# Four instead of three buffers for gathered rows, and three fewer key units computed ahead, in the expert layer of a fused two-block kernel

## The chip, the cores and the metric

One Trainium2 chip, one of its cores. The metric is the device time of one execution in microseconds; lower is better. The engines are named as the profile names them: PE multiplies matrices (PEld is its weight load), DVE works on vectors, ACT computes activations and copies, POOL issues the gathers here, SP issues the plain loads from memory.

## The reference

The program is a hybrid block (pooling and forgetting attention), a second block of two attentions, and then an expert layer (PEER) over 512 tokens of width 1024. All that the change touches lies in the expert layer, which is, cut to what matters:

```python
def block(xt):                                   # 128 tokens at a time
    q = (xt @ w_q).reshape(128, 8, 2, 128)
    sc = einsum('thcd,chnd->thcn', q, sub_keys)  # 8 heads, 2 x 128 sub-keys
    ...                                          # top 16 of each, top 16 of their sums
    g = softmax(best_s)                          # 8 x 16 experts of 16384 per token
    pre = einsum('td,thkd->thk', xt, u[idx])
    coef = g * gelu(pre)
    return einsum('thk,thkd->td', coef, v[idx])
```

`u` and `v` are tables of 16384 rows of 1024 numbers.

## The kernel before

The expert layer treats its tokens in two ways, side by side.

**The first 128 tokens** take their expert rows by gathers. For each of the 128 selected slots, `gather_load` (L1613) lets POOL issue an indirect load of one row of `u` or of `v` per token (128 rows of 4 KB, 512 KB) into a tile `gat`. `gather_step` (L1622) lets DVE use it: a `u` row is multiplied with the token and summed (L1631, into `pre`), a `v` row is scaled and added to `acc` (L1635). That makes 256 gathers and 256 DVE steps. The list `items` alternates `v` and `u` after the first 24 `u`. A step that has used its tile issues the next load at once, so that as many gathers are under way as `gat` has buffers; a load waits until the DVE step that last used its buffer is done.

**The other 384 tokens** are computed against all 16384 experts, 128 experts to a unit. A *u stage* (`u_stage`, L1395) is 24 PE matmuls of 384 columns, in three passes over a high and a low part of the operands; ACT applies Gelu (`u_gelu`, L1445) and leaves the result in a *slot*, a tile of 128 x 384 numbers. A *v stage* (`v_half`, L1717, twice) multiplies the unit's weights with the `v` rows: 18 matmuls of 512 columns, added up in six banks over all 128 units. Ahead of each stage `prep` (L1378) splits the loaded tile into its high part on ACT (L1389: `uhi`, `h_hi`, `vhi`) and its low part on DVE (L1390: `ulo`, `h_lo`, `vlo`), and has SP load the next tile (L1364). Two sets of tiles take turns, so the same work shows as `uhi`/`ulo` and as `h_hi`/`h_lo`.

The program's order is written by hand. Each engine runs its instructions in that order.

1. *Routing* (until about 963 us): queries, top-16 searches, and in between 22 of the u stages, then 3 more.
2. *One-hots* (about 972 to 1119 us): 24 blocks (`one_hots` L1649 on DVE: `aa`, `oh` and two `bb`; `products` L1662 on PE: 32 small matmuls, copied by ACT) build a table of gate weights `Gd` in memory. A block may hold one u stage; the number per block follows from `left`, what is still to be computed ahead.
3. Five further u stages, each with a gather step.
4. *The main loop* (L1739, about 1140 to 2010 us): 128 turns, each with one v stage. `NU` u stages are done ahead of it, the other 128 - `NU` inside, in the turns that `u_at` lists (at most one per turn, from turn 5 to turn 122). This is the loop, cut:

```python
gdue = float(after)                       # after = 5 gather steps are done
for s in range(128):
    if s in u_at:
        o = u_stage(u_at[s])
    gdue += 2.9 if s in u_at else 0.75
    if s + 1 in u_at:
        prep("u", u_at[s + 1], V)
    ...                                   # gate_load every 8 turns; w_mult, prep("v"), w_split for turn s + 1
    if s in u_at:
        u_gelu(u_at[s], o)
    v_half(s, 0)
    while gi["use"] < min(int(gdue), len(items)):
        gather_step()
    v_half(s, 1)
```

So DVE's order in a turn is: the low part for the next u stage, the weights (L1705, L1712) and the low part for the next v stage, and then the gather steps that have come due. `gate_load` (L1699) has SP fetch 1.5 MB of `Gd` for eight turns. The slots are `NU` in number: 10 `Gx`, 10 `Gm`, 16 `Gn`, `Gq`, two PSUM banks and three parts of a gate tile. `Gq` and `gat` lie in one pool (`pQ`) in SBUF. After the loop the rows of the other 384 tokens are read back (`xr`, in `gat`'s buffers) and added to the banks.

Of the kernel before, what the change touches and what calls it, by code (L numbers as in the profile page):

```python
# [10 lines left out]
F32 = mybir.dt.float32  # L11
# [12 lines left out]
D = 1024  # L24
# [36 lines left out]
def hybrid_mla_peer_kernel(ctx: ExitStack, tc: tile.TileContext, x, meta, gains, rows, bforget, wf, w1v, w1u, poolw,  # L61
# [13 lines left out]
    def bank(tag, bufs):  # L75
        return ps.tile([128, 512], F32, name=tag, tag=tag, bufs=bufs)
# [1241 lines left out]
    ND = T - 128  # L1318
# [17 lines left out]


    FIRST = 5
    NU = 20 + 16 + 13 + FIRST
    ahead_of = list(range(FIRST, NU)) + list(range(FIRST))  # L1340
    LEAD = 122
    done = [min(128, NU + (max(0, s + 2 - FIRST) * (128 - NU)) // (LEAD + 2 - FIRST)) for s in range(128)]
    u_at = {s: done[s] - 1 for s in range(128) if done[s] > (done[s - 1] if s else NU)}
    assert all(done[s] >= min(128, s + 4) for s in range(128)) and len(u_at) == 128 - NU
    VA = 1
# [49 lines left out]
    def u_stage(j):  # L1395
        o = mm_bank()
        hi, lo = uw.pop(j)
        for k in range(KD):
            mm3(o[:, :ND], (hi[:, k, :], lo[:, k, :]), (h3[0][:, k, 128:T], h3[1][:, k, 128:T]), k == 0, k == KD - 1)
        return o  # L1400
# [38 lines left out]
    slots = [Gx[:, i, :] for i in range(10)] + [Gm[:, i, :] for i in range(10)]  # L1439
# [3 lines left out]
    def u_gelu(j, o):  # L1443
        gl[j] = slots.pop(0)
        S.activation(gl[j], o[:, :ND], AF.Gelu)  # L1445

    def run_ahead(n, eng):
        for _ in range(n):
            i = ua["n"]
            ua["n"] += 1  # L1450
            if i + 1 < NU:
                prep("u", ahead_of[i + 1], eng)
# [138 lines left out]
        by_slot(tt)  # L1591
    cR.close()
    pQ = ctx.enter_context(tc.tile_pool(name="pQ", bufs=1))
    Gq = pQ.tile([128, 13, ND], F32, name="Gq", tag="Gq")
    slots.extend(Gq[:, i, :] for i in range(13))
    slots.extend(bank(tag, 1)[:, :ND] for tag in ("av", "mi"))


# [14 lines left out]
    def gather_load():  # L1613
        if gi["load"] < len(items):
            kind, s = items[gi["load"]]
            t = pQ.tile([128, D], F32, name="gat", tag="gat", bufs=3)
            G.indirect_dma_start(out=t, out_offset=None, in_=peer_u if kind == "u" else peer_v,  # L1617
                                 in_offset=bass.IndirectOffsetOnAxis(ap=idx[:, s:s + 1], axis=0))
            gt[gi["load"]] = t
            gi["load"] += 1  # L1620

    def gather_step():  # L1622
        i = gi["use"]
        if i >= len(items):
            return
        kind, s = items[i]
        while gi["load"] <= i:
            gather_load()
        t = gt.pop(i)
        if kind == "u":  # L1630
            V.tensor_tensor_reduce(t, t, xt0, 1.0, 0.0, op0=OP.mult, op1=OP.add, accum_out=pre[:, s:s + 1])  # L1631
            if s % 16 == 15:
                ripe.append((i + LATE, s // 16))
        else:
            V.scalar_tensor_tensor(acc, t, pre[:, s:s + 1], acc, op0=OP.mult, op1=OP.add)  # L1635
        gi["use"] += 1
        gather_load()
        if ripe and ripe[0][0] <= i:
            h = ripe.pop(0)[1]
            c = pre[:, 16 * h:16 * h + 16]  # L1640
            S.activation(c, c, AF.Gelu)
            V.tensor_tensor(c, c, gg0[:, h, :], op=OP.mult)

    for _ in range(3):
        gather_load()


# [29 lines left out]
    n_b = ND // NB  # L1677
    left = NU - after - ua["n"]
    for b in range(n_b + 1):
# [16 lines left out]
    def gate_load(q):  # L1696
        if q < 128 // GJ:
            gates[q] = tV([128, ND // NB, GJ * NB], "gate", bufs=2)
            nc.sync.dma_start(gates[q], Gd[q])  # L1699

    def w_mult(j):
        g = gates[j // GJ].rearrange("p b (j t) -> p b j t", j=GJ)[:, :, j % GJ, :]
        x = gl.pop(j)
        xv = x.rearrange("p (b t) -> p b t", t=NB)
        V.scalar_tensor_tensor(xv, xv, 1.0 / 16384.0, g, op0=OP.mult, op1=OP.mult)  # L1705
        return x

    def w_split(j, x):
        hi = tV([128, ND], "w_hi", F32R, bufs=2)
        lo = tV([128, ND], "w_lo", F32R, bufs=2)  # L1710
        S.activation(hi, x, AF.Copy)  # L1711
        V.tensor_tensor(lo, x, hi.bitcast(F32), op=OP.subtract)  # L1712
        if j >= FIRST:
            slots.append(x)
        return hi, lo

    def v_half(j, n):  # L1717
        hi, lo = vw[j]
        w = ws[j]
        c = slice(512 * n, 512 * n + 512)  # L1720
        for tt in range(3):
            mm3(ob[2 * tt + n], (w[0][:, tok(tt)], w[1][:, tok(tt)]), (hi[:, c], lo[:, c]), j == 0, j == 127)
        if n == 1:
            vw.pop(j), ws.pop(j)
# [13 lines left out]
    gdue = float(after)  # L1738
    for s in range(128):  # L1739
        nx = s + VA  # L1740
        if s in u_at:
            o = u_stage(u_at[s])
        gdue += 2.9 if s in u_at else 0.75
        if s + 1 in u_at:
            prep("u", u_at[s + 1], V)
        if nx < 128:
            if nx == FIRST or nx % GJ == 0:
                gate_load(nx // GJ + 1)
            wg = w_mult(nx)
            prep("v", nx, V)  # L1750
            ws[nx] = w_split(nx, wg)
# [6 lines that stand above are left out]
# [2 lines left out]
        gather_step()  # L1760
    xr = []
    for tt in range(3):
        xr.append(pQ.tile([128, D], F32, name="xr", tag="gat", bufs=3))
        nc.scalar.dma_start(xr[tt], x2d[tt])
    nc.scalar.dma_start(out[0:128, :], acc)
    for n in range(2):
# [81 lines left out]
```

## Time and profile before

| what | value |
|---|---|
| time, median of 3 runs | 2022.4 us (2020.04 to 2023.79) |
| the profiled execution's own time | 2023.68 us |
| its span, first to last instruction | 2020.9 us |
| PE busy | 1951.3 us, 97% |
| DVE busy | 1370.9 us, 68% |
| ACT busy | 770.8 us, 38% |
| POOL busy | 619.5 us, 31% |
| granted TensorE clock, mean | 0.986 |

A busy PE is not a PE at its peak: the profile models the ends of matmuls, which overlap. What a stage of matmuls takes is therefore read from the starts of the first one of it and of the next stage, and what PE loses from the idle time ahead of an instruction and from the clock. Granted clock 1.0 is 2.4 GHz, 0.5 is 1.2 GHz.

### The profile page before, as it was taken

What the parts mean: (1) busy time and instruction counts of PE and PEld (TensorE: products, weight loads), DVE (VectorE), ACT (ScalarE), POOL (GpSimd) and SP (SyncE); (2) the same over time, 40 slices, a digit from 0 to 9 for tenths busy, and PEclk for the clock granted to TensorE, in tenths of its full rate; (3) what the DMA queues carried; (4) which work ended last, traced back from release to release, by engine and by line L of the source; (5) the groups of instructions that cost most, each with busy time, mean ns of one, the idle gap of its engine ahead of it and who ended that gap; (6) DMA issues with size and microseconds to landing.
All of it is one profiled execution on the core that took longest, in us unless ns stands there. A gap on an engine that the chain in (4) does not pass through costs nothing.

```text
span 2020.9 us, 26905 instructions
## 1 busy us (share of the span) xinstructions
PE 1951.3 (97%) x10297; PEld 1669.7 (83%) x10297; DVE 1370.9 (68%) x2571; ACT 770.8 (38%) x1228; POOL 619.5 (31%) x479
## 2 busy tenths in 40 slices
PE   7999999999997989999999999999999999999998
PEld 5777688877886779889999888888888888888887
DVE  4233423564576668999899677777787777777686
ACT  4223323254575442223565433333333333333332
POOL 1001100200147015655100134434444444433442
PEclk9999999999999999999999999999999999999999
DMA  4211122322111133213789888888888888888885
GB/s 156 92 63 42 42 84 96 133 92 73 36 54 63 42 133 108 94 42 105 231 260 264 277 321 319 315 304 296 321 288 304 302 310 292 313 318 306 282 293 205
DMA packets 138129, 387.63 MB, mean 192 GB/s; under 512 B 10624, under 2 KB 59904, under 8 KB 129808
## 3 DMA queue, kind: packets, MB, share of 16 engines
q1 hardware_dynamic: 48576, 216.65, 30.4%
q0 software_dynamic: 36864, 134.23, 19.4%
q10 hardware_dynamic: 52560, 35.03, 5.9%
q8 instruction: 80, 1.31, 0.3%
q14 instruction: 49, 0.40, 0.1%
HBM read 357.04 MB, written 28.84 MB: 191 GB/s over the span
## 4 chain that ended last, share of the span: by engine, by line
PE 51%; DMA 22%; issue 10%; DVE 9%; POOL 6%; ACT 2%; DVEq 0%; POOLq 0%; ACTq 0%; SPq 0%
DMA gat<-in_peer_v,idx 12%; DMA gat<-in_peer_u,idx 9%; PE mm L150 9%; PE mm L152 9%; PE mm L151 9%; POOL gat L1617 4%; DVE acc L1635 2%; PE s L151 2%; PE s L152 2%; PE s L150 2%; PE pt L151 2%; PE pt L152 2%; PE pt L150 2%; PE av L1044 1%; PE s L561 1%
## 5 line engine op out<-in xcount | busy, mean ns | idle before, releaser
L1617 POOL DMA_INDIRECT gat<-in_peer_u,idx x128 | 203.1, 1586 | 413.2 <-DVE pre L1631 207.0
L1617 POOL DMA_INDIRECT gat<-in_peer_v,idx x128 | 172.6, 1348 | 233.6 <-DVE pre L1631 137.5
L1631 DVE CUSTOM_DVE_ANT_0 gat<-gat,xt 128x1024 f32<-128x1024 f32 x128 | 156.0, 1221 | 102.3 <-DMA gat<-in_peer_u,idx 102.2
L1635 DVE SCALAR_TENSOR_TENSOR acc<-gat,pre,acc 128x1024 f32<-128x1024 f32 x128 | 164.2, 1283 | 83.3 <-DMA gat<-in_peer_v,idx 82.8
L152 PE MATMUL mm<-h_hi,ulo 128*128 128x384 f32 x568 | 192.5, 339 | 7.3 <-DVE ulo L1390 5.9
L150 PE MATMUL mm<-h_hi,uhi 128*128 128x384 f32 x568 | 193.4, 340 | 0.0
L151 PE MATMUL mm<-h_lo,uhi 128*128 128x384 f32 x568 | 191.9, 338 | 0.0
L130 DVE TENSOR_TENSOR wlo<-wraw,whi 128x2048 fp32r<-128x2048 f32 (+1 forms) x42 | 96.1, 2289 | 135.3 <-ACT whi L129 135.2
L152 PE MATMUL mm<-h_hi,h_lo 128*128 128x384 f32 x456 | 156.8, 344 | 16.4 <-DVE h_lo L1390 13.9
L1389 ACT ACTIVATE vhi<-xt 128x1024 fp32r<-128x1024 f32 x97 | 102.7, 1058 | 181.9 <-issue 112.8
L150 PE MATMUL mm<-h_hi 128*128 128x384 f32 x456 | 157.0, 344 | 0.0
L151 PE MATMUL mm<-h_lo,h_hi 128*128 128x384 f32 x456 | 155.6, 341 | 0.0
L129 ACT ACTIVATE whi<-wraw 128x2048 fp32r<-128x2048 f32 (+2 forms) x53 | 97.5, 1841 | 110.9 <-PE mm L151 59.0
L1390 DVE TENSOR_TENSOR vlo<-xt,vhi 128x1024 fp32r<-128x1024 f32 x97 | 118.4, 1221 | 23.2 <-ACT vhi L1389 22.8
L152 PEld LDWEIGHTS mm<-h_hi,ulo 128*128 128x128 f32 x568 | 107.7, 190 | 9.3 <-DVE ulo L1390 7.2
L150 PEld LDWEIGHTS mm<-h_hi,uhi 128*128 128x128 f32 x568 | 107.6, 190 | 1.8
L151 PEld LDWEIGHTS mm<-h_lo,uhi 128*128 128x128 f32 x568 | 107.7, 190 | 1.7
L150 PE MATMUL mm<-hT_hi,whi 128*128 128x512 f32 x256 | 104.7, 409 | 1.3 <-DVE fz L417 1.0
L150 PE MATMUL s<-vhi,w_hi 128*128 128x512 f32 x256 | 100.0, 391 | 4.5 <-ACT w_hi L1711 4.5
L152 PEld LDWEIGHTS mm<-h_hi,h_lo 128*128 128x128 f32 x456 | 87.8, 192 | 19.6 <-DVE h_lo L1390 16.6
L152 PE MATMUL mm<-hT_hi,wlo 128*128 128x512 f32 x256 | 102.2, 399 | 0.0
L151 PE MATMUL mm<-hT_lo,whi 128*128 128x512 f32 x256 | 102.1, 399 | 0.0
(586 smaller groups left out, 5062.4 us busy)
## 6 DMA issues: line engine op xcount, KB each, us to landing
xt<-in_peer_v SPq DMA_DIRECT2D x97, 512.0 KB, 5.6
xt<-in_uT SPq DMA_DIRECT2D x95, 512.0 KB, 4.8
Gd<-stage ACTq DMA_DIRECT2D x24, 1024.0 KB, 5.3
gate<-Gd SPq DMA_DIRECT2D x16, 1536.0 KB, 10.4
raw<-in_uT SPq DMA_DIRECT2D x33, 512.0 KB, 4.9
wraw<-in_w1u SPq DMA_DIRECT2D x16, 1024.0 KB, 4.8
raw<-in_peer_v SPq DMA_DIRECT2D x31, 512.0 KB, 5.5
wraw<-in_wpq SPq DMA_DIRECT2D x8, 1024.0 KB, 4.8
```

Of the source, the lines that this page charges most:

```text
L129: S.activation(hi[:, :n], r[:, :n], AF.Copy)
L130: lo_eng["e"].tensor_tensor(lo[:, :n], r[:, :n], hi[:, :n].bitcast(F32), op=OP.subtract)
L150: PE.matmul(o, L[0], R[0], start=start, stop=False)
L151: PE.matmul(o, L[0], R[1], start=False, stop=False)
L152: PE.matmul(o, L[1], R[0], start=False, stop=stop)
L561: PE.matmul(s[:, :w], qT[pr, h // 2, tok(qt)], kT[pr, h // 2, n0:16 + n], start=True, stop=False)
L1044: PE.matmul(av[:, col(h, qt):col(h, qt) + 64], pts[i][:, c + j * 128:c + (j + 1) * 128], src[:, j, h * 64:(h + 1) * 64], start=(j == 0), s ...
L1389: S.activation(hi, src, AF.Copy)
L1390: eng.tensor_tensor(lo, src, hi.bitcast(F32), op=OP.subtract)
L1617: G.indirect_dma_start(out=t, out_offset=None, in_=peer_u if kind == "u" else peer_v, in_offset=bass.IndirectOffsetOnAxis(ap=idx[:, s:s + ...
L1631: V.tensor_tensor_reduce(t, t, xt0, 1.0, 0.0, op0=OP.mult, op1=OP.add, accum_out=pre[:, s:s + 1])
L1635: V.scalar_tensor_tensor(acc, t, pre[:, s:s + 1], acc, op0=OP.mult, op1=OP.add)
```

## The change

```diff
-    NU = 20 + 16 + 13 + FIRST
+    NU = 20 + 16 + 10 + FIRST
...
-    Gq = pQ.tile([128, 13, ND], F32, name="Gq", tag="Gq")
-    slots.extend(Gq[:, i, :] for i in range(13))
+    Gq = pQ.tile([128, 10, ND], F32, name="Gq", tag="Gq")
+    slots.extend(Gq[:, i, :] for i in range(10))
...
-            t = pQ.tile([128, D], F32, name="gat", tag="gat", bufs=3)
+            t = pQ.tile([128, D], F32, name="gat", tag="gat", bufs=4)
...
-    for _ in range(3):
+    for _ in range(4):
         gather_load()
...
-        gdue += 2.9 if s in u_at else 0.75
+        gdue += 2.9 if s in u_at else 0.6
...
-        xr.append(pQ.tile([128, D], F32, name="xr", tag="gat", bufs=3))
+        xr.append(pQ.tile([128, D], F32, name="xr", tag="gat", bufs=4))
```

`gat` gets a fourth buffer of 4 KB per partition. `Gq` gives up three slots of 1.5 KB each for it, so 51 units instead of 54 are computed ahead and 77 instead of 74 u stages lie in the main loop. A turn without a u stage brings 0.6 instead of 0.75 gather steps. With `NU` = 54 all 24 one-hot blocks hold a u stage; with 51, three of them (the first, the ninth and the seventeenth) hold none.

DVE at the first one-hot block, where `g` are the gate weights of the tokens, in the change's order against that before:

```order
 L1588 SCALAR_TENSOR_TENSOR g_5759<-pt,g_5759 128x256
 L1588 SCALAR_TENSOR_TENSOR g_5759<-s,g_5759 128x256
+L1656 TENSOR_TENSOR aa<-I_5757,iota 128x2048
+L1657 TENSOR_TENSOR oh<-J_5758,iota 128x2048
+L1659 TENSOR_TENSOR bb<-oh,g_5759 128x2048 x2
 L1390 TENSOR_TENSOR ulo<-xt,uhi 128x1024
 L1656 TENSOR_TENSOR aa<-I_5757,iota 128x2048
```

The first block's `aa`, `oh` and `bb` now come without a `ulo` ahead of them; the same three rows without a `ulo` stand at the ninth and the seventeenth block.

ACT at the same place, from the last u stage ahead of the blocks on (`Gn<-mm` is `u_gelu`, the four copies and the load to `Gd` are `products`), before:

```order
L1445 ACTIVATE Gn<-mm 128x384
L1389 ACTIVATE h_hi<-raw 128x8x128
L1445 ACTIVATE Gn<-mm 128x384
L1671 COPY stage<-s 128x128x4
L1671 COPY stage<-pt 128x128x4
L1671 COPY stage<-s 128x128x4
L1671 COPY stage<-pt 128x128x4
L1672 DMA Gd<-stage 128x16x128
L1389 ACTIVATE uhi<-xt 128x1024
```

and in the change:

```order
L1445 ACTIVATE Gn<-mm 128x384
L1671 COPY stage<-s 128x128x4
L1671 COPY stage<-pt 128x128x4
L1671 COPY stage<-s 128x128x4
L1671 COPY stage<-pt 128x128x4
L1672 DMA Gd<-stage 128x16x128
L1389 ACTIVATE h_hi<-raw 128x8x128
L1445 ACTIVATE Gn<-mm 128x384
```

One split (`h_hi`) and the Gelu of one u stage stood ahead of the first block's copies and now stand behind them, so one u stage fewer lies ahead of the first `products`.

DVE in turns 10 and 11 of the main loop, from `w_mult` (L1705) of turn 10 on, before:

```order
L1705 SCALAR_TENSOR_TENSOR Gx<-Gx,gate 128x384
L1390 TENSOR_TENSOR vlo<-xt,vhi 128x1024
L1712 TENSOR_TENSOR w_lo<-Gx,w_hi 128x384
L1631 ISA gat,pre<-gat,xt 128x1024
L1631 ISA pre 128x1
L1631 ISA gat,pre<-gat,xt 128x1024
L1631 ISA pre 128x1
L1631 ISA gat,pre<-gat,xt 128x1024
L1631 ISA pre 128x1
L1390 TENSOR_TENSOR ulo<-xt,uhi 128x1024
L1705 SCALAR_TENSOR_TENSOR Gx<-Gx,gate 128x384
L1390 TENSOR_TENSOR vlo<-raw,vhi 128x1024
```

and in the change, from the split for turn 11's u stage on:

```order
L1390 TENSOR_TENSOR h_lo<-xt,h_hi 128x8x128
L1705 SCALAR_TENSOR_TENSOR Gx<-Gx,gate 128x384
L1390 TENSOR_TENSOR vlo<-raw,vhi 128x1024
L1712 TENSOR_TENSOR w_lo<-Gx,w_hi 128x384
L1631 ISA gat,pre<-gat,xt 128x1024
L1631 ISA pre 128x1
L1631 ISA gat,pre<-gat,xt 128x1024
L1631 ISA pre 128x1
L1631 ISA gat,pre<-gat,xt 128x1024
L1631 ISA pre 128x1
L1705 SCALAR_TENSOR_TENSOR Gx<-Gx,gate 128x384
L1390 TENSOR_TENSOR vlo<-xt,vhi 128x1024
```

Turn 11 has a u stage in the change and had none before, so its `h_lo` stands in turn 10 now; the next u stage after turn 10 was that of turn 12, whose `ulo` came behind turn 10's three gather steps. POOL issues the same gathers in the same order. What differs there is the DVE step that a gather's buffer waits for: the third step before it until now, the fourth with the change.

## Rows read from the trace of the kernel before

**Rows 1.** The page, part 4: the chain that ended last, by line.

```profile
DMA gat<-in_peer_v,idx 12%; DMA gat<-in_peer_u,idx 9%; PE mm L150 9%; PE mm L152 9%; PE mm L151 9%; POOL gat L1617 4%; DVE acc L1635 2%; PE s L151 2%; PE s L152 2%; PE s L150 2%; PE pt L151 2%; PE pt L152 2%; PE pt L150 2%; PE av L1044 1%; PE s L561 1%
```

**Rows 2.** Busy time by stretch; last columns clock, DMA share, GB/s.

```profile
core 0: us, PE busy (x) PEld busy (x) DVE busy (x) ACT busy (x) POOL busy (x), PEclk, DMA share, GB/s
1140.00:2010.00 870.00, 845.62 (x4062) 746.12 (x4061) 655.71 (x839) 300.79 (x411) 367.76 (x249) 0.99 0.85 298
985.00:1110.00 125.00, 125.00 (x1167) 121.86 (x1165) 122.32 (x106) 75.09 (x126) 0.00 (x0) 1.00 0.92 263
```

**Rows 3.** Waits of PE, main loop: total us, times, longest.

```profile
PE mm L152 <- DVE h_lo L1390: 13.9, 8, 3.0
PE mm L152 <- DVE ulo L1390: 5.9, 4, 2.5
PE s L150 <- ACT w_hi L1711: 4.5, 3, 3.0
```

**Rows 4.** The same view for DVE, 1155 to 2010 us.

```profile
DVE gat L1631 <- DMA gat<-in_peer_u,idx: 102.2, 47, 8.3
DVE acc L1635 <- DMA gat<-in_peer_v,idx: 82.8, 48, 6.0
```

**Rows 5.** The tile gat, 1155 to 2010 us: idle time until, and landing.

```profile
  DVE acc L1635: 225.6, 87
  DVE pre L1631: 172.4, 58
...
DMA to landing us min/median/max: 4.1/6.2/13.6
```

**Rows 6.** Timelines of DVE, SP, POOL and PE, 1447 to 1468 us.

```profile
1447.87 1.29 DVE L1635 SCALAR_TENSOR_TENSOR acc<-gat,pre,acc 128x1024 f32<-128x1024 f32 x1 [0.44 <-DMA gat<-in_peer_v,idx]
...
1452.31 0.60 SPq L1699 DMA_DIRECT2D gate<-Gd  x1
...
1453.78 1.01 POOL L1617 DMA_INDIRECT gat<-in_peer_v,idx  x1 [2.21 <-DMA gat<-in_peer_v,idx]
...
1465.15 1.28 DVE L1635 SCALAR_TENSOR_TENSOR acc<-gat,pre,acc 128x1024 f32<-128x1024 f32 x1 [6.04 <-DMA gat<-in_peer_v,idx]
...
1467.63 0.55 PE L152 MATMUL mm<-h_hi,h_lo 128*128 128x384 f32 x1 [3.04 <-DVE h_lo L1390]
```

**Rows 7.** Busy time by stretch: a gate load, three clock spells.

```profile
1453.00:1465.00 12.00, 11.59 (x56) 9.83 (x54) 5.11 (x8) 3.04 (x5) 2.87 (x3) 1.00 1.02 414
1116.20:1119.60 3.40, 3.40 (x26) 3.40 (x24) 0.00 (x0) 2.42 (x5) 0.00 (x0) 0.51 0.72 207
1362.00:1365.40 3.40, 3.40 (x13) 3.40 (x12) 3.40 (x6) 1.03 (x2) 1.39 (x1) 0.50 0.86 298
1915.00:1918.40 3.40, 3.40 (x9) 2.51 (x9) 2.88 (x5) 1.82 (x2) 1.39 (x1) 0.50 0.79 266
```

**Rows 8.** Timeline of PE: starts of v, u and v stage.

```profile
1701.40 0.39 PE L150 MATMUL s<-vhi,w_hi 128*128 128x512 f32 x1
...
1705.52 0.33 PE L150 MATMUL mm<-h_hi,uhi 128*128 128x384 f32 x1
...
1709.70 0.39 PE L150 MATMUL s<-vhi,w_hi 128*128 128x512 f32 x1
```

**Rows 9.** Timelines of PE and DVE in one one-hot block.

```profile
1052.75 0.42 PE L150 MATMUL mm<-h_hi 128*128 128x384 f32 x1
...
1055.29 1.23 DVE L1390 TENSOR_TENSOR ulo<-xt,uhi 128x1024 fp32r<-128x1024 f32 x1
...
1056.43 1.22 DVE L1656 TENSOR_TENSOR aa<-I,iota 128x2048 f16<-128x2048 f16 x1
...
1061.31 1.23 DVE L1390 TENSOR_TENSOR h_lo<-xt,h_hi 128x1024 fp32r<-128x1024 f32 x1
```

**Rows 10.** Timeline of PE, the last one-hot block.

```profile
1114.34 0.23 PE L1670 MATMUL s<-bb,aa 128*128 128x128 f16 x1 [1.14 <-DVE bb L1659]
```

**Rows 11.** The page, part 6: one load, KB each, us to landing.

```profile
gate<-Gd SPq DMA_DIRECT2D x16, 1536.0 KB, 10.4
```

## Prediction

> **What bounds the kernel now.** I read the chain of waits first. A quarter of the chain that ended last is the gathers: their transfers 21%, their issue on POOL 4%; the rest of its large entries is matmuls [rows 1]. So two things are near a limit in the main loop, and the busy time by stretch says which: PE is busy for 845.6 of 870 us [rows 2]. PE sets the loop, and the gathers cost time only where they make PE wait. Who waited for whom on PE names those places: 15 waits, 13.9 + 5.9 + 4.5 = 24.3 us, all for the low or high part of an operand (`h_lo`, `ulo`, `w_hi`), none longer than 3.0 us [rows 3]. DVE makes those parts, and the same view for DVE shows it waiting 102.2 + 82.8 = 185 us for the gathers' landing [rows 4]. Most of the 185 us is free, because DVE works about one turn ahead of PE; 24.3 us of it come through.
>
> One event shows how [rows 6]. At 1452.31 SP issues the gate load (1.5 MB, 10.4 us to land [rows 11]). At 1453.78 POOL issues a gather; it lands 11.3 us later, where the median is 6.2 and the longest 13.6 [rows 5]. DVE waits 6.04 us for it at 1465.15, does `h_lo` only then, and PE has waited 3.04 us. In that stretch the DMA engines are full (share 1.02, 414 GB/s) [rows 7], while over the loop they move 298 GB/s at a share of 0.85 [rows 2]. So a late gather is one whose transfer falls into the queue behind a gate load, and there is one such load per eight turns.
>
> A wait on PE costs twice. After the longer ones the granted clock is at 0.50, the 1.2 GHz level, for 3.4 us; six such spells lie in the loop, the first and the last of them in [rows 7]. Half of 3.4 us is lost in each: 6 x 1.7 = 10.2 us. What the gathers cost now is 24.3 + 10.2 = 34.5 us.
>
> **The change, part by part.**
>
> *The fourth buffer.* A gather waits for the DVE step that last used its buffer; POOL waited 225.6 + 172.4 = 398 us for such steps in 145 waits [rows 5], so the buffers, not POOL, set when a gather starts. A turn with a u stage takes 1705.52 - 1701.40 = 4.1 us for the v stage and 1709.70 - 1705.52 = 4.2 us for the u stage [rows 8], 8.3 us in all, and has about three gather steps. With three buffers, and three steps in the turn before as well, each gather is issued when the same step of that turn is done, so it has 8.3 us to land. With four, the first of the three has a whole turn more, and the other two have one DVE step more (1.3 us, the length of the step in [rows 6]), about 9.6 us. DVE's lead adds 6.04 - 3.04 = 3.0 us before PE feels it [rows 6]. So PE waited where a landing took over 11.3 us, and will where it takes over 12.6. Many gathers gain more than 1.3 us: the one of 1453.78 would have had its buffer when the step of 1447.87 ended, at 1449.16, ahead of the gate load instead of behind it. Against that, the longest landing of 13.6 us still exceeds 12.6, and one more gather under way makes each somewhat slower. Bounds: none of the 34.5 us goes (the queue is full anyway), or all. I take 20 of the 24.3 us, leaving 4.3 us or about 0.3 us for each of the 16 gate loads, and five of the six clock spells, 8.5 us: -28.5 us.
>
> A rule of the Trainium skill speaks against this: "DMA: Bandwidth & Descriptors", section "Issuing engines are not separate DMA queues", says that transfers started by any engine run on the same 16 DMA engines and interleave there. By that a fourth gather adds a request and no bandwidth, and the sum would be that of the first rival below. The trace agrees inside a gate load (share 1.02) but leaves 15% of the engines' time free over the loop.
>
> *Three more u stages in the loop.* 77 instead of 74, each 4.2 us of a PE that has no free time there [rows 8]: 3 x 4.18 = +12.5 us. Their loads, 3 x 0.5 MB, are 0.6% of what the loop moves (298 GB/s for 870 us is 259 MB). DVE has 656 us of work in 870 us [rows 2], so three more `ulo` of 1.2 us are covered.
>
> *Three u stages fewer among the one-hot blocks.* There PE (125.0 of 125 us) and DVE (122.3) are both full [rows 2]. A block takes 1061.31 - 1055.29 = 6.02 us; its `ulo` takes 1056.43 - 1055.29 = 1.14 us of DVE's time [rows 9]. Without u stage DVE needs 6.02 - 1.14 = 4.9 us and PE only 6.02 - 4.2 = 1.8 us, so PE stands idle about 3.1 us and the block is DVE's. The 12.5 us of PE that go to the loop thus come back here only as 3 x 1.14 = -3.4 us. And the idle PE may lose its clock: in the last block, where it waited 1.14 us and again soon after [rows 10], the clock fell to 0.51 for 3.4 us [rows 7]. If that follows each of the three blocks, 1.7 us are lost each time in a PE that is full, 3 x (1.7 - 1.14) = +1.7 us. Between -3.4 and +1.7 I take -1.0, a little above the middle towards the loss, because waits of this length did bring the spell.
>
> *The pace of the gathers.* Before, 5 + 74 x 2.9 + 54 x 0.75 = 260.1 steps come due by the last turn; now 5 + 77 x 2.9 + 51 x 0.6 = 258.9. Both pass 256, in turn 122 before and 123 now, with four turns of 4.1 us behind it as cover; if it slipped past the last turn, each step left over would cost 1.3 us at the end. Nothing. But a turn without u stage now has mostly no gather step where it had one, which leaves its 4.1 us for landing. That is in the 20 us above.
>
> *The rest.* A fourth gather at the start and `xr` in one of four buffers change no wait that PE or the end sees: POOL has nothing else to do between those first gathers and the first gather step, and the `xr` loads stand behind ACT's last split as before. Nothing.
>
> Sum: -28.5 + 12.5 - 1.0 = **-17.0 us**. On the profiled execution's own 2023.7 us that is 2006.7; that execution lies 1.3 us above the median of the runs shown, and 2022.4 - 17.0 = **2005.4 us**.
>
> **The rivals.**
>
> *The transfers bind, not the buffers (14%).* In a gate load the DMA engines are full [rows 7], so a fourth gather queues behind the same bytes and gains only its 1.3 us. For it: the waits come in those stretches. Against it: a gather issued 4 us earlier stands ahead of the gate load, and the queue does run empty in between. Half of the 34.5 us would go: -17.2 + 12.5 - 1.0 = -5.7, **2016.7 us**.
>
> *Slower: the moved u stages outweigh (10%).* This is the one mechanism of the three units alone: PE's 12.5 us leave a place where DVE pays for most of them and go to a place where PE pays for all. It decides as soon as the fourth buffer takes back less than 12.5 - 1.0 = 11.5 us, a third of the 34.5, for instance if the denser u turns make the row loads on SP late instead of the gathers. With nothing taken back: +11.5, **2033.9 us**; with the clock lost in all three blocks, 2036.6.
>
> *The change does not do what it says (4%).* If POOL's issue itself were late, a free buffer would help nothing. Its issue takes 4% of the chain [rows 1] against 398 us of waiting for buffers [rows 5], so I see little for it; the time would be the same 2033.9 us.
>
> *All of it goes (a part of the likeliest case).* -34.5 + 12.5 - 3.4 = -25.4, 1997.0 us.
>
> **How the numbers follow.** The forecast has 72%, with its own range 1997 to 2013; the rivals 14, 10 and 4%. The predicted time is the forecast's, 2005.4 us. The range for 8 in 10 takes in the first rival with a few us around it and leaves the slower cases out, 1997 to 2021. What a measurement of this kernel tells from no change is about 0.2%, 4 us: faster means below 2018.4. Faster: 72% and most of the first rival, 0.81. Within 0.2%: the rest of it and a weak gain, 0.07. Slower: 0.12, nearly all of the last two rivals.
>
> **What would show it.** In the profile after: PE's waits in the loop near 4 us instead of 24.3, at most one or two clock spells of 3.4 us there, and DVE's waits for gathers well under the 185 us. 77 u stages in the loop; the time from the first to the last matmul of the loop shorter by about 28.5 - 12.5 = 16 us. Three one-hot blocks of about 4.9 us in which PE idles about 3 us, each perhaps followed by a clock of 0.5. The prediction is wrong if PE's waits in the loop stay above some 15 us although POOL no longer waits for the third step back (the first rival), if new waits for the row loads on SP appear, or if the one-hot stretch does not get shorter.

## The result and the profile after

The changed kernel took 1996.0 us (median of four runs, 1994.2 to 1998.5), beside 2021.2 us (2018.7 to 2023.8) for the kernel before in the same session: ratio 0.9876, 95% interval 0.9857 to 0.9895, 25 us less. Forecast were 17 us less, 2005.4 us; the range of 1997 to 2021 ends 1 us above the measured median. In a later session the ratio was 0.9842 (0.9815 to 0.9869).

The page of the profile after, part 1 (busy time of each engine) and the first line of part 4 (the chain that ended last):

```profile
span 1995.2 us, 27005 instructions
## 1 busy us (share of the span) xinstructions
PE 1943.4 (97%) x10297; PEld 1668.0 (84%) x10297; DVE 1370.7 (69%) x2571; ACT 768.6 (39%) x1228; POOL 590.9 (30%) x479
...
PE 92%; DVE 3%; POOL 2%; ACT 2%; issue 1%; DMA 1%; ACTq 0%; SPq 0%; DVEq 0%; POOLq 0%
```

The gathers, a quarter of the chain before [rows 1], have left it: DMA and POOL together hold 3%, and the chain is PE's.

Busy time by stretch, the loop and the one-hot blocks of the profile after (columns as in [rows 2]):

```profile
1140.00:1989.00 849.00, 848.62 (x4156) 754.72 (x4154) 661.43 (x845) 302.44 (x418) 338.22 (x248) 1.00 0.87 309
985.00:1110.00 125.00, 120.93 (x1124) 117.36 (x1123) 118.34 (x102) 72.50 (x122) 0.00 (x0) 0.97 0.88 252
```

PE's clock is 1.00 over the whole loop. Who waited for whom has no row for PE in this stretch, where [rows 3] had 24.3 us in 15 waits. For DVE the same view says, in us in total, times, longest:

```profile
DVE vlo L1390 <- ACT vhi L1389: 163.5, 99, 3.6
DVE gat L1631 <- DMA gat<-in_peer_u,idx: 11.2, 9, 3.3
...
DVE acc L1635 <- DMA gat<-in_peer_v,idx: 1.2, 3, 0.8
```

Of the 185 us of [rows 4] 12.4 are left. What DVE waits for instead is `vhi`. It has two tiles, so ACT can write one only when PE has read that of two v stages earlier; ACT starts 0.09 us after the end of that stage in 125 of 126 turns. DVE now runs as far ahead of PE as the tiles of the v stage allow.

**Where the 25.8 us of the spans come from** (2020.9 to 1995.2 us):

| stretch | before | after | difference |
|---|---|---|---|
| up to the first one-hot block's first DVE instruction | 972.8 | 972.4 | -0.4 |
| from there to the first v matmul | 166.9 | 168.0 | +1.1 |
| the loop, first v matmul to the end of the last | 874.7 | 848.2 | -26.5 |
| to the end of the span | 6.6 | 6.5 | 0.0 |

The loop's ends are the starts of two matmuls on PE's timeline of the profile after, the second plus its 0.39 us:

```profile
1140.40 0.39 PE L150 MATMUL s<-vhi,w_hi 128*128 128x512 f32 x1
...
1988.23 0.39 PE L152 MATMUL mi<-vhi,w_lo 128*128 128x512 f32 x1
```

### The profile page after: what moved, and what is told of

Same layout as the page of the kernel before. It is cut to its first block, busy times and chain, and to the rows that moved or that the text cites. A ratio compares the mean times of both kernels' runs of the same rounds, so it can differ in the third digit from the quotient of the medians.

```text
span 1995.2 us, 27005 instructions
## 1 busy us (share of the span) xinstructions
PE 1943.4 (97%) x10297; PEld 1668.0 (84%) x10297; DVE 1370.7 (69%) x2571; ACT 768.6 (39%) x1228; POOL 590.9 (30%) x479
## 4 chain that ended last, share of the span: by engine, by line
PE 92%; DVE 3%; POOL 2%; ACT 2%; issue 1%; DMA 1%; ACTq 0%; SPq 0%; DVEq 0%; POOLq 0%
PE mm L150 15%; PE mm L152 14%; PE mm L151 14%; PE s L151 4%; PE s L152 4%; PE pt L151 4%; PE pt L152 4%; PE s L150 4%; PE pt L150 4%; PE mi L150 2%; PE mi L152 2%; PE mi L151 2%; PE av L151 1%; PE av L152 1%; PE av L150 1%; PE av L1044 1%
## 5 line engine op out<-in xcount | busy, mean ns | idle before, releaser
L1617 POOL DMA_INDIRECT gat<-in_peer_u,idx x128 | 162.3, 1268 | 409.6 <-DVE pre L1631 373.8
L1617 POOL DMA_INDIRECT gat<-in_peer_v,idx x128 | 184.2, 1439 | 234.6 <-DVE acc L1635 211.6
L152 PE MATMUL pt<-vhi,w_lo 128*128 128x512 f32 x256 | 100.2, 392 | 0.0
L152 PE MATMUL s<-vhi,w_lo 128*128 128x512 f32 x256 | 100.2, 392 | 0.0
```

The costliest lines, as they stand in the source:

```text
L152: PE.matmul(o, L[1], R[0], start=False, stop=stop)
```

## The experiments

Fourteen runs follow: thirteen other kernels, and the changed one again. The table gives for each the loop, read as above from its profiled execution, and what of it was lost to waits. A loop in which PE never waits is known from the runs: 835.5 us with 74 u stages (the run with the buffer alone), 844.0 with 76, 848.2 with 77, 856.7 with 79. That is 4.23 us for a u stage, and (835.5 - 74 x 4.23) / 128 = 4.08 us for a v stage. "Lost" is the loop less the wait-free one of the same number of u stages. (The 45.5 and 31.8 us in the expectations were taken against the pitch of the matmuls; 6.5 us of such a number are there in a loop without waits too.) The ratio is to the kernel before, which ran beside each. The loop is that of a single execution: the one of pace_30_06 lies 6.4 us above that kernel's median, the one of pace_27_10 5.6 us above, the one of pace_alone 3.2 us below, so with three buffers some 6 us between two losses say little.

| kernel | buffers, units ahead | loop us | lost us | median us | ratio (95%) |
|---|---|---|---|---|---|
| before | 3, 54 | 874.7 | 39.2 | 2021.2 | |
| changed | 4, 51 | 848.2 | 0 | 1996.0 | 0.9876 (0.9857 to 0.9895) |
| changed_again | 4, 51 | 848.2 | 0 | 1993.6 | 0.9842 (0.9815 to 0.9869) |
| units_alone | 3, 51 | 873.5 | 25.3 | 2021.9 | 0.9998 (0.9982 to 1.0014) |
| buffer_alone | 4, 54 | 835.5 | 0 | 1982.9 | 0.9800 (0.9783 to 0.9818) |
| pace075 | 4, 51 | 848.2 | 0 | 1994.8 | 0.9851 (0.9837 to 0.9866) |
| four_nu52 | 4, 52 | 844.0 | 0 | 1991.8 | 0.9835 (0.9819 to 0.9851) |
| five_buffers | 5, 49 | 856.7 | 0 | 1999.2 | 0.9880 (0.9862 to 0.9899) |
| no_u_last | 4, 51 | 848.2 | 0 | 1990.4 | 0.9840 (0.9822 to 0.9857) |
| pieces_before | 3, 54 | 856.6 | 21.1 | 2005.5 | 0.9896 (0.9866 to 0.9926) |
| pace_alone | 3, 54 | 843.4 | 7.9 | 2011.1 | 0.9949 (0.9930 to 0.9968) |
| pace_30_06 | 3, 54 | 876.0 | 40.5 | 2019.8 | 0.9971 (0.9953 to 0.9989) |
| pace_27_10 | 3, 54 | 860.8 | 25.3 | 2002.0 | 0.9885 (0.9857 to 0.9914) |
| pieces_and_pace | 3, 54 | 850.8 | 15.3 | 2000.5 | 0.9866 (0.9836 to 0.9896) |
| fewer_gathers | 3, 54 | 836.2 | 0.7 | 1984.0 | 0.9816 (0.9801 to 0.9830) |
| two_buffers | 2, 54 | 1040.7 | 205.2 | 2192.0 | 1.0856 (1.0833 to 1.0879) |

### The parts of the change, each alone

**Units alone.**

```diff
-    NU = 20 + 16 + 13 + FIRST
+    NU = 20 + 16 + 10 + FIRST
-    Gq = pQ.tile([128, 13, ND], F32, name="Gq", tag="Gq")
+    Gq = pQ.tile([128, 10, ND], F32, name="Gq", tag="Gq")
```

> The kernel before with 51 instead of 54 units ahead (ten slots in `Gq`), still three gather buffers and 0.75 steps in a turn without u stage. Theory (the units cost and the fourth buffer gives): PE's waits and clock spells in the loop stay (45.5 us of lost PE time there, with the 4 us of slow matmuls around them, 35 to 50 here), the three u stages cost 12.5 us and the one-hot blocks 0.7 us: 2021.2 + 13.2 = about 2034 us, ratio to before 1.0065. Rival (the new spread of the u stages over the turns, and not the buffer, took the waits away): the loop loses under 15 us and the time is 2034 - 30 = about 2004 us or less.

Neither the theory nor the rival came out. The kernel is as fast as before, 0.9998. Who waited for whom, PE, its loop:

```profile
PE mm L152 <- DVE ulo L1390: 10.2, 5, 3.0
PE mm L152 <- DVE h_lo L1390: 5.6, 5, 1.9
```

That is 15.8 us instead of 24.3, with three clock spells instead of six in the loop. Three more u stages are 12.7 us more of PE's work, and 13.9 us less were lost. With three buffers the moved work costs nothing: in these two executions it fills time that PE would have waited. Why the waits shrink by just that much is not shown. That is not a slower kernel, as the prediction's second rival had it, and no saving either.

**The buffer alone.** The fourth buffer lies where `I2`, `J2` and `g2` were, so that no slot has to go (shown without the lines that make those three views of one tile `sel`):

```diff
-            t = pQ.tile([128, D], F32, name="gat", tag="gat", bufs=3)
+            n = gi["load"] % 4
+            if n not in gb:
+                gb[n] = pQ.tile([128, D], F32, name="gat", tag="gat", bufs=3) if n < 3 else sel[:, :2 * D].bitcast(F32)
+            t = gb[n]
```

> The kernel before with a fourth gather buffer and nothing else: 54 units ahead, 0.75 steps in a turn without u stage. The fourth buffer is taken from the space of `I2`, `J2` and `g2`, which nothing uses after the last one-hot block, so no slot is given up for it; it is there from the end of the one-hot blocks on. Theory (the fourth buffer ends the waits by itself, and each of the three u stages costs its 4.2 us once no wait is left for it to fill): lost PE time in the loop falls from 45.5 to under 8 us, ratio to before 0.981, about 1982 to 1985 us, 12 us below the changed kernel. Rival (buffer and units need each other: 74 u stages in the loop leave the transfers too little time, as 31.8 us instead of 45.5 us were lost with 77 u stages and three buffers): 10 to 20 us of loss stay and the ratio is 0.986 to 0.991, the same as the changed kernel or worse.

The theory's ratio was 0.981; 0.9800 came, with no wait of PE in the loop, 39.2 us of loss gone, and 11 to 13 us below the changed kernel. So the whole gain of the change is the buffer's, and with four buffers the three u stages cost what they take, 12.7 us. This is the version that beats both kernels; its five runs lie between 1981.5 and 1983.0 us.

The event of [rows 6] in this kernel: the same gathers at the same gate load, on the timelines of POOL, SP and DVE.

```profile
1434.68 1.29 POOL L1622 DMA_INDIRECT gat<-in_peer_v,idx  x1 [0.31 <-issue]
...
1438.24 0.43 SPq L1704 DMA_DIRECT2D gate<-Gd  x1
1439.71 1.01 POOL L1622 DMA_INDIRECT sel<-in_peer_u,idx  x1 [3.74 <-DVE pre L1636]
...
1444.64 1.28 DVE L1640 SCALAR_TENSOR_TENSOR acc<-gat,pre,acc 128x1024 f32<-128x1024 f32 x1
...
1454.69 1.22 DVE L1636 CUSTOM_DVE_ANT_0 sel<-sel,xt 128x1024 f32<-128x1024 f32 x1
```

The gather that was issued 1.5 us behind the gate load (1453.78 against 1452.31) is now issued 3.6 us ahead of it, and DVE uses it 10 us later without a wait, where it waited 6.04 us. Now the gather after it stands 1.5 us behind the gate load (1439.71, into the fourth buffer `sel`); DVE uses that one 15 us later, without a wait too.

**The pace, with four buffers.**

```diff
-        gdue += 2.9 if s in u_at else 0.6
+        gdue += 2.9 if s in u_at else 0.75
```

> The changed kernel with 0.75 instead of 0.6 gather steps in a turn without u stage, so with the fourth buffer and 51 units. Theory (the buffer does it): PE's waits in the loop stay under 5 us and the time within 4 us of the changed kernel's 1996.0. Rival (the slower pace is what let the gathers land in time): single gather steps in turns without u stage bring back 10 to 25 us of waits, 2006 to 2021 us.

1994.8 us and no wait of PE: with four buffers the pace does nothing.

**One unit back, and a fifth buffer.**

```diff
-    NU = 20 + 16 + 10 + FIRST
+    NU = 20 + 16 + 11 + FIRST    # four_nu52; five_buffers: 8, bufs=5
```

> The changed kernel with 52 units ahead (eleven slots in `Gq`, the most that fits beside four buffers). Theory (each unit in the loop costs its 4.2 us of PE, and no wait is left for the loop's transfers): 1996.0 - 4.2 - 0.2 = about 1991.6 us, ratio to before 0.9853. Rival (the transfers are near their limit in the loop, so that a shorter loop only brings waits): 1995 us or more, with over 3 us of PE waits in the loop.

> The changed kernel with five gather buffers and 49 units ahead (eight slots in `Gq`). Theory (the fourth buffer left nothing to gain, and each unit moved into the loop costs its 4.2 us of PE there and gives back little among the one-hots): lost PE time in the loop stays at 6.5 us and the time is 1996.0 + 2 x 4.2 = about 2004 us, ratio 0.9915. Rival (DVE's last 20 us of waits for gathers still cost something that the fifth buffer takes): 2001 us or less.

The first came out as its theory said, 1991.8 us, and no wait came back. The second is slower than the changed kernel of its neighbour sessions by 3 to 6 us where 8 were expected. Its 1999.2 us lie in the range of the rival, but not for the rival's reason: its loop is longer by exactly two u stages (856.7 against 848.2) and loses nothing, and its one-hot stretch, with five blocks without u stage, gives a part back (161.0 us from its first DVE instruction to the first v matmul, 168.0 in the profile after; 10.2 against 17.1 us of that at half clock). A fifth buffer has nothing left to take.

**The one-hot blocks without u stage moved to the end.**

```diff
-        if NU - after - ua["n"] > left - min(left, left * (b + 1) // n_b):
+        if b < left:
```

> The changed kernel, but the three one-hot blocks without a u stage are the last three instead of the first, the ninth and the seventeenth. Theory (each of the three places costs a spell at half clock, 1.7 us of a PE that is full right after): one or two spells instead of four, and 2 to 5 us less than the changed kernel, 1991 to 1994 us, ratio 0.985 to 0.9865. Rival (DVE bounds the stretch and the spells are hidden in it): the same as the changed kernel within 1 us; or, PE being idle three times in a row, the clock stays low into the five u stages behind the blocks: 1 to 3 us more.

1990.4 us, 0.6 us below the range that its theory gave. Busy time by stretch of the four spells at half clock among the one-hots of the profile after, then, of this kernel, its one spell, as long as the longest of the four:

```profile
976.30:983.10 6.80, 5.93 (x40) 5.92 (x39) 6.76 (x7) 3.40 (x5) 0.00 (x0) 0.50 0.74 249
1020.60:1024.10 3.50, 3.50 (x31) 3.50 (x29) 3.46 (x4) 2.34 (x4) 0.00 (x0) 0.51 0.81 234
1068.40:1071.80 3.40, 3.40 (x33) 3.40 (x31) 3.37 (x4) 1.98 (x4) 0.00 (x0) 0.50 0.89 248
1116.20:1119.60 3.40, 3.40 (x32) 3.40 (x32) 0.00 (x0) 1.76 (x3) 0.00 (x0) 0.50 0.93 263
```

```profile
1104.50:1111.30 6.80, 5.30 (x50) 4.88 (x48) 6.73 (x7) 3.59 (x7) 0.00 (x0) 0.50 0.73 212
```

The stretch from the first one-hot block to the first v matmul is 161.2 us here, 168.0 in the profile after and 166.9 before. 17.1 us at half clock cost 8.5 us of a full PE in the profile after, 6.8 us cost 3.4 here; the difference would explain 5.1 of the 6.8 us. In the total the gain over the changed kernel is 3 to 6 us against the two sessions of that kernel, which did not run beside it; the intervals of the ratios touch, so the total alone does not settle it.

### Why three buffers lose so much

**Gate loads in pieces, three buffers.**

```diff
-            if nx == FIRST or nx % GJ == 0:
-                gate_load(nx // GJ + 1)
+            if nx == FIRST:
+                gate_load(nx // GJ + 1)
+            elif nx >= GJ:
+                gate_piece(nx // GJ + 1, nx % GJ)    # a sixth of it in each of six turns
```

> The kernel before (three buffers, 54 units), but each gate load of 1.5 MB from the second on is issued as six loads of 0.25 MB, one in each of six turns. Theory (the gathers that PE waited for are those queued behind one whole gate load): PE's waits fall from 24.3 to under 8 us, most of the 38.8 us come back without the three u stages in the loop, 1983 to 1992 us. Rival (three buffers are too few whatever the other loads do, since each gather has only a turn to land): 15 us of waits or more stay, 2010 to 2022 us.

Between the two: 21.1 of 39.2 us are still lost. PE's waits in the loop of this kernel:

```profile
PE mm L152 <- DVE ulo L1390: 6.5, 6, 2.2
PE mm L152 <- DVE h_lo L1390: 6.3, 7, 1.7
PE s L150 <- ACT w_hi L1717: 1.6, 2, 0.8
```

So whole gate loads are behind about half of the loss, and the other half is there when the same bytes come in pieces.

**The pace, three buffers.** Three kernels that differ from the one before in one line:

```diff
-        gdue += 2.9 if s in u_at else 0.75
+        gdue += 2.9 if s in u_at else 0.6     # pace_alone
+        gdue += 3.0 if s in u_at else 0.6     # pace_30_06
+        gdue += 2.7 if s in u_at else 1.0     # pace_27_10
```

> The kernel before with 0.6 instead of 0.75 gather steps in a turn without u stage, three buffers and 54 units. The sum of due steps is 252, so four steps are left for after the loop, at 1.3 us each. Theory (the pace does nothing by itself): lost PE time in the loop stays within 8 us of 45.5, the last steps cost up to 5 us, ratio 0.997 to 1.003. Rival (single steps in turns without u stage are what shortens the time that the next gathers have): the loss falls to 30 us or less, ratio 0.995 or less.

> The kernel before (three buffers, 54 units) with 3.0 gather steps in a turn with u stage and 0.6 in one without. All 256 steps come due in the loop, the last in turn 122 as before, so the rate is the same; turns without u stage that hold a single step are 29 instead of 36. Theory (a single step in a short turn is what starts the next gathers late, so with three buffers the spread of the steps over the turns decides how much is lost): lost PE time in the loop near the 14.3 us of the run with 0.6 alone and nothing left after the loop, about 1988 to 1996 us, ratio 0.983 to 0.987. Rival (0.6 alone lost less only because it asked for 3% fewer steps in the loop and paid for four of them behind it): the loss stays at 30 to 45 us, ratio 0.993 to 1.000.

> The same kernel with 2.7 and 1.0 steps, so the other way: 52 turns without u stage hold a single step, and 23 turns with u stage two instead of three. Theory (single steps in short turns are what makes gathers late): lost PE time rises above 45.5 us, 50 to 70 us, ratio 1.003 to 1.015. Rival (the rate alone counts, or steps spread more evenly help): loss of 45 us or less, ratio 1.000 or less.

The first, pace_alone, came out as its rival had it (0.9949), so I took the rival's reason over: a single gather step in a short turn is what makes the next gathers late. That fell twice, and both runs came out as their rivals had it. With the fewest single steps (pace_30_06) nothing was gained in the profiled loop and 0.3% in the median; with the most (pace_27_10) it was 14 us and 1.1%. In order of the loss the three go by how soon all steps are asked for: the last comes due in turn 122 before and with 3.0 and 0.6 (39.2 and 40.5 us lost), in turn 125 with 2.7 and 1.0 (25.3 us lost), and with 0.6 alone four of the 256 are not asked for at all within the loop (7.9 us lost). That this order is the cause is argued, not shown: units_alone asks soonest of all, its last step in turn 119, and lost 25.3 us, and pace_27_10 also spreads its steps most evenly. pace_alone then pays behind the loop: from its last matmul to the end of the span 18.4 us pass instead of 6.6, since the leftover gathers have to land before the `xr` loads can use their buffers.

**Pieces and pace together, three buffers.** The edit is that of pieces_before with the pace of pace_30_06.

> Three buffers, 54 units, gate loads in six pieces and the pace 3.0 and 0.6 together. Theory (late gathers come from two things, the whole gate load ahead of them and the single steps that start them late; the fourth buffer covers both): lost PE time under 10 us, ratio 0.980 to 0.983, the same as the fourth buffer alone. Rival (three buffers leave too little time in any case): 14 us or more of loss, ratio 0.985 or more.

15.3 us are lost, 0.9866: as the rival had it (14 us or more, 0.985 or more). These two together did not do what the buffer does.

**A theory of the rate.** The buffers are a ring. In the trace before, a buffer that comes free holds a landed gather 7.4 us later on average (from the end of the DVE step that frees it to the landing, over the 249 gathers issued in the loop), and the step takes 1.25 us: 8.65 us, or one gather each 2.9 us with three buffers. The loop asks for 251 steps until turn 122, which is 123 x 4.08 + 74 x 4.23 = 815 us without waits, one each 3.25 us, and in the turns with a u stage 2.9 steps in 8.3 us, one each 2.9. Three buffers are at their limit in those turns and have little left elsewhere; a landing that takes 13 us [rows 5] is not made up, and the next gathers are late too. With four it is one each 2.2 us (in changed_again the 7.4 us are 7.7, which gives 2.2 as well). Two kernels test it.

```diff
-            t = pQ.tile([128, D], F32, name="gat", tag="gat", bufs=3)
+            n = gi["load"] % 2        # two_buffers
+            if n not in gb:
+                gb[n] = pQ.tile([128, D], F32, name="gat", tag="gat", bufs=3)
+            t = gb[n]
```

> The kernel before with two gather buffers instead of three, nothing else. Theory (the buffers are a ring with a rate of its own: from a free buffer to the landing 7.4 us on average, and 1.25 us for the step, so three buffers give a gather each 2.9 us at best, where the loop wants one each 3.2 us and the turns with a u stage one each 2.8 us; with two, landing perhaps 0.7 us faster, it is one each 4.0 us): the loop becomes 251 x 4.0 = about 1000 us plus the last turns, the time 2150 to 2230 us, and DVE waits for most of the gathers, not only for those behind a gate load. Rival (only gathers queued behind one of the 16 gate loads are late; each is late by one more step of 3.4 us, with a clock spell of 1.7 us): 16 x 5.1 = 82 us more, 2100 us or less.

2192.0 us, inside the theory's range and 92 us above the rival's limit. Who waited for whom in its loop, DVE and PE:

```profile
DVE acc L1639 <- DMA gat<-in_peer_v,idx: 194.8, 79, 8.5
DVE gat L1635 <- DMA gat<-in_peer_u,idx: 170.5, 67, 7.6
PE mm L152 <- DVE ulo L1390: 55.3, 20, 6.8
PE mm L152 <- DVE h_lo L1390: 51.9, 20, 5.4
PE s L150 <- ACT w_hi L1715: 26.4, 10, 7.1
```

146 of the 256 gathers were waited for, and the steps lie 4.0 us apart (from DVE's steps) where 4.0 were expected. That figure took the landing as 0.7 us faster than with three buffers; with 7.4 us it would have been 4.3. The run bears the faster one out: 2 x 4.0 - 1.25 leaves at most 6.8 us from a free buffer to the landing. The DMA engines are at 0.73 of their time in this loop, so it is not they that are full.

```diff
+    items = items[:242]
-        gdue += 2.9 if s in u_at else 0.75
+        gdue += 2.7 if s in u_at else 0.7
```

> The kernel before (three buffers, 54 units) with 242 instead of 256 gathers and steps (the last 14 of the `v` rows of the first 128 tokens are left out) and the pace set to 2.7 and 0.7, so that they are spread over the whole loop: one each 3.5 us instead of 3.2. All 16 gate loads stay whole. Theory (three buffers are just short of the rate that is asked of them, so a rate 8% lower ends most of the waits): the loop is within 10 us of the wait-free 835.5 us, 1982 to 1994 us, ratio 0.980 to 0.986. Rival (what is late is what stands behind a whole gate load, and there are as many of these): 25 us or more are lost in the loop, 2007 us or more, ratio 0.993 or more.

1984.0 us, as by the theory. With three buffers and all gate loads whole, PE's only row in the loop, and DVE's:

```profile
DVE gat L1632 <- DMA gat<-in_peer_u,idx: 46.0, 29, 4.5
DVE acc L1636 <- DMA gat<-in_peer_v,idx: 33.2, 23, 4.6
PE mm L152 <- DVE h_lo L1390: 0.5, 1, 0.5
```

Asked for one gather each 3.5 us instead of 3.25, and 2.7 instead of 2.9 in a turn with u stage, three buffers do. (It leaves work out: 14 gathers and steps, 18 us of DVE in a loop where DVE has some 190 us free; this is not what ended PE's waits.)

**The changed kernel again**, beside the last pace runs:

> The changed kernel once more beside these, for a ratio of the same rounds: 0.986 to 0.989. Both theories expect no wait of PE in the loop, three one-hot blocks without u stage, and 6.5 us of lost PE time.

The ratio is 0.9842, below the range expected: this kernel took 2.3 us less than in the first session and the kernel before 3.9 us more. The loop is the same to 0.1 us, with no wait of PE. Landing of the tile `gat` in this kernel's loop, to be read against [rows 5], and the busy time by stretch of one gate load, against the first row of [rows 7]:

```profile
DMA to landing us min/median/max: 4.5/6.8/12.0
```

```profile
1500.00:1510.00 10.00, 10.00 (x51) 8.96 (x50) 7.85 (x11) 4.39 (x6) 2.45 (x3) 1.00 0.94 352
```

A gather takes 0.6 us longer than before, not less. Nothing about the transfers got faster; there is more time to wait for them.

## Why the prediction was off, point by point

**What bounds the kernel, and where its loss comes from: right.** PE's waits, DVE's late low parts and the late gathers were one chain: with the fourth buffer all three are gone together, and in buffer_alone nothing else was changed.

**The fourth buffer, -28.5 us: the step that failed, in its size.** It measured -39.2 us (buffer_alone), and in the changed kernel 26.5 + 12.7 = -39.2 as well. 10.7 us were missing, in two pieces.

- The prediction kept 4.3 us of waits and one clock spell (1.7 us), because "the longest landing of 13.6 us still exceeds 12.6". The 12.6 took the gain of a gather with one buffer more as 1.3 us, one DVE step. On average it is the distance from one step to the next, 3.3 us: from the end of the releasing step to the moment when DVE wants the gather the median went from 8.2 to 11.4 us (worked out from DVE's rows in the traces of before and after). Of the 249 gathers issued in the loop before, 98 landed after DVE wanted them, by up to 8.3 us; in changed_again it is 17 of 248, by at most 1.6 us, less than the 3.0 us of DVE's lead. The prediction also treated gathers as late one by one behind gate loads. That is where PE's waits began in the trace before (20.8 of the 24.3 us within 20 us of a gate load's issue). But without whole gate loads 21.1 of 39.2 us stayed lost (pieces_before), and with all of them whole 0.7 us were lost at a lower rate (fewer_gathers). The ring's rate fits both: near its limit lateness is carried on, and where the ring has room, it is not.
- What the waits cost now was put at 24.3 + 10.2 = 34.5 us. They cost 39.2. The other 4.7 us, 0.3 us for each of the 15 waits, are around the waits; that they lie in matmuls that start again slowly is argued, not shown.

**Three more u stages in the loop, +12.5 us: right with four buffers** (12.7, or 4.23 us each, over four counts of units). With three it is zero, because there the work fills waits; so the prediction's sum holds only in the order buffer first, units after.

**One-hot blocks, -1.0 us: within the bounds of -3.4 to +1.7.** From the first block to the first v matmul it was +1.1 us in the profile after, -2.0 in that of changed_again, 0.0 in pace075. The saving of DVE's time is there, and the clock spells take it back: the three have 17.1, 10.2 and 13.7 us at half clock in this stretch, the trace before 3.4.

**The pace and the rest, nothing: right** with four buffers.

**The rivals.** *The transfers bind*: refused; in the 10 us behind a gate load's issue the DMA engines are as full as before (mean share 0.98 over the 16 loads, in the trace before and in that of changed_again), and the gain came all the same. A rule that the prediction set beside it, of the Trainium skill, "DMA: Bandwidth & Descriptors", section "Issuing engines are not separate DMA queues", says that transfers interleave on the same 16 engines whoever starts them. By it a fourth gather brings no bandwidth. The traces agree: a gather lands later after its issue (6.8 against 6.2 us), and 309 instead of 298 GB/s are nearly the same bytes in a shorter loop. What it left open is that the kernel was short of gathers under way, not of bandwidth. *The moved u stages outweigh*: refused, 0.9998 for them alone. *The change does not do what it says*: refused by [rows 6] against buffer_alone's timeline. *All of it goes*: this is what happened to the loop. Its sum of -25.4 us is what was measured, but by other terms: -39.2 instead of -34.5 for the waits and +0.7 instead of -3.4 up to the loop.

**Open:** units_alone lost 25.3 us with three buffers though its steps are asked for slightly faster than before, so something beside the rate counts, perhaps the spread of the steps over the turns; these runs do not explain it.

## What to carry to other kernels

Buffers of a stream of transfers are a ring: (time from free buffer to landing + time of use) / buffers is the shortest distance at which it delivers. Set that beside the distance at which the loop asks, in its densest stretch; here, where the two were near, one buffer more was worth the whole loss, and where there was room, none. An engine that waits can have room for moved work at no cost, as here with three buffers; once the wait is gone, the same work has its full price, so price two parts of a change in both orders.

## What was not expected

The times of the kernels with three buffers scatter much more than those with four: the one before ran from 2015.4 to 2033.5 us in one session, buffer_alone from 1981.5 to 1983.0. What makes the difference between executions of one kernel is not shown. And half-clock spells among the one-hot blocks follow two waits of about 1 us each: PE's timeline of the profile after, ahead of the spell at 1020.6 us, the waits in brackets:

```profile
1019.14 0.23 PE L1670 MATMUL s<-bb,aa 128*128 128x128 f16 x1 [1.13 <-DVE bb L1659]
1020.27 0.59 PE L1670 MATMUL s<-bb,aa 128*128 128x128 f16 x7 [0.90 <-DVE bb L1659]
```

One small matmul stands between the two waits. In the kernel four_nu52, with two such blocks and 4.9 us of the same waits in five places, the clock shows no spell at all between 762 and 1987 us, and in changed_again one of four such places has none; why they are spared stays open.
